# The triangular inversion inside a gated DeltaNet: 32-row substitution on VectorE, or 16-row substitution joined by small matmuls

## Chip, cores and metric

One of the eight cores of a Trainium2 chip runs the whole program. The metric is the device time of one execution in microseconds (us). Engines are named as the profile names them: PE is TensorE's matmul side and PEld its weight loads, DVE is VectorE, ACT ScalarE, POOL GpSimd, SP SyncE. PE, DVE, ACT and POOL each work through their own queue strictly in the order of the program; semaphores tie the queues together.

## The reference, cut to what matters

Two layers of a diffusion transformer over 512 latent and 256 context tokens. In each layer one half of the mixer is a gated DeltaNet with 8 heads, run forwards and backwards over chunks of 64 tokens. Each chunk, head and direction needs the solution of a unit lower triangular system of 64 rows:

```python
a_mat = jnp.where(strict, jnp.einsum('bhnid,bhnjd->bhnij', kb, k) * decay, 0.0)
eye = jnp.eye(CHUNK, dtype=jnp.float32)
rhs = jnp.concatenate([v * beta[..., None], kb * jnp.exp(gc)[..., None]], axis=-1)
sol = lax.linalg.triangular_solve(a_mat + eye, rhs, left_side=True, lower=True)
```

The kernel forms the inverse of `a_mat + eye` and multiplies with it. The other half of the mixer is latent attention; projections and a SwiGLU FFN surround both, for the context and the latent tokens.

## The kernel before

Each layer is written as several Python generators: input projection, the DeltaNet chain, the preparation and the body of attention, output projection with FFN, modulation. `weave` is a planner that picks which generator goes on next: every `yield` gives a span, a PE cost and a DVE cost, `TUNE` gives each stream a rank and a factor on those costs, and from them the order of all engines' instructions is fixed when the program is built. Nothing is reordered at run time.

`gdn_pre` prepares the DeltaNet for 16 units (head pair by chunk) in both directions. It runs six times: once over the context in each layer, and twice over the latent tokens in each layer (heads 0 to 3, then 4 to 7). Call these inversions 1 to 6; in order of time they are context layer 0, latent layer 0 twice, context layer 1, latent layer 1 twice. A tile holds on its 128 partitions four quarters of 32 rows (two heads, two 32-row diagonal blocks of the 64-row matrix) and along the free axis 32 units (16 units, two directions). The inversion goes so:

- The diagonal 32-blocks are gathered in `bd`, transposed to `L` (line 568), and `M` starts as the identity.
- The loop of lines 571 to 576 substitutes row by row: for `r` from 0 to 30, one multiply makes an outer product of `n` = 31 - r by `m` = r + 1 elements in `tmp` (shown as `st<-g,g`), one subtract takes it from `M` (shown as `g<-g,st`). That is 62 DVE instructions, all through the helper `tt` of line 139, each of which needs the one before it.
- Two transposes (lines 578, 579) turn `M` into `x1` and `x2`.
- Small matmuls of 32 x 32 (lines 587, 588, then 597, 598) join the two 32-blocks to a 64-block: 64 matmuls into one PSUM bank, a copy on ACT, 64 matmuls into another bank. Then come the products with values and keys (line 622) and the scan over chunks.

PSUM banks with the tag `B` hold these products; there are two, and attention's scores (line 961) use the same two. On PE the streams interleave: lines 221 and 226 are the projections and the FFN, 232 modulation and attention's output, 933, 938 and 946 the preparation of attention, whose maxima DVE reduces in lines 934 and 939. DVE also splits each weight tile in two (`wl<-wr,wh`, `fl<-fr,fh`). ACT runs every `cpy` and `act` through line 151.

Of the kernel before, what the change touches and what calls it, by code (L numbers as in the profile page):

```python
# [14 lines left out]
AF = mybir.ActivationFunctionType  # L15
# [5 lines left out]
P = 128  # L21
# [10 lines left out]
GROUPS = ((0, 4), (4, 4), (8, 4), (12, 4), (16, 3), (19, 3))  # L32
SLOT = 776

C_ID, C_BLK1, C_TRIF, C_TRIB, C_SEL, C_MSK, C_ONE, C_BLKM, C_QB = 0, 128, 256, 384, 512, 520, 524, 525, 527
NCONST = 529
B_MOD, N1, N2, CW, AL, DT, GN, QN, KN, FN = 0, 48, 56, 64, 124, 132, 140, 141, 143, 144
NSMALL = 152

# [66 lines left out]
def trunk_kernel(ctx, tc, xin, cc, wmod, small, win, wuq, wuk, wuv, wout, wgu, wdn, cst, rope, out):  # L106
    nc = tc.nc
    V, A, G, PE = nc.vector, nc.scalar, nc.gpsimd, nc.tensor
# [14 lines left out]
    def nm(s):  # L123
        uid[0] += 1
        return f"{s}_{uid[0]}"

    def slot(tag, dt=F32, w=None):
        width = WIDTH[tag]
        t = sp.tile([P, width], dt, name=nm(tag), tag=tag, bufs=BUFS[tag])
        return t[:, 0:w or width]  # L130

    def ps(tag):
        return pp.tile([P, 512], F32, name=nm("ps" + tag), tag=tag, bufs=PSB[tag])
# [4 lines left out]
    def tt(out, a, b, op=ALU.mult, e=None):  # L138
        (e or V).tensor_tensor(out=out, in0=a, in1=b, op=op)  # L139
# [7 lines left out]
    def stt(out, a, s, b, op0, op1):  # L147
        V.scalar_tensor_tensor(out=out, in0=a, scalar=s, in1=b, op0=op0, op1=op1)  # L148

    def act(out, a, f, **kw):  # L150
        A.activation(out, a, f, **kw)  # L151
# [4 lines left out]
    MUL, ADD, SUB = ALU.mult, ALU.add, ALU.subtract  # L156

    cct = cp.tile([P, KD, 2], F32, name="cct")
    nc.sync.dma_start(out=cct, in_=cc)
    cst_t = cp.tile([P, NCONST], F32, name="cst")  # L160
    nc.sync.dma_start(out=cst_t, in_=cst)
# [7 lines left out]
    sel = cst_t[:, C_SEL:C_SEL + 8]  # L169
    m0 = cst_t[:, C_MSK:C_MSK + 1]  # L170
    m1 = cst_t[:, C_MSK + 1:C_MSK + 2]
    nm0 = cst_t[:, C_MSK + 2:C_MSK + 3]
    nm1 = cst_t[:, C_MSK + 3:C_MSK + 4]
    ident_r = cp.tile([P, P], F32R, name="ident_r")
# [2 lines left out]
    for l in range(DEPTH):  # L177
        t = cp.tile([P, NSMALL], F32, name=f"small{l}")
# [266 lines left out]
    def st_tile():  # L445
        return slot("st")

    def u3(t):
        return t.rearrange("p (c i) -> p c i", i=64)
# [3 lines left out]
    def gdn_pre(l, st, hjs, kf, qf, vf, gt, res):  # L453
# [16 lines left out]
        for d in range(2):  # L470
            t = gb[d]
# [6 lines left out]
        def turned(f, a):  # L478
            pt = ps("B")
            for c in range(8):  # L480
                for hp in range(2):
                    s = slice(64 * hp, 64 * hp + 64)
                    PE.matmul(pt[s, 64 * c:64 * c + 64], u3(f)[s, a + c, :], ident[s, s], start=True, stop=True)
            return pt

        for a in (0, 8):
            pt = turned(kf, a)
# [20 lines left out]
        for a in (0, 8):  # L508
            pt = turned(vf, a)
# [20 lines left out]
        if full:  # L530
# [3 lines left out]
            pt = ps("B")  # L534
# [5 lines left out]
        for b in range(0, U, nb):  # L540
            pt = ps("B")
            pv = pt.rearrange("p (c z i) -> p c z i", z=nz, i=64)
# [14 lines left out]
        bd, L, M = (slot("g4") for _ in range(3))  # L557
# [4 lines left out]
        b3 = bd.rearrange("p (u i) -> p u i", i=32)  # L562
# [3 lines left out]
        V.transpose(out=bd[:, 512:1024], in_=bt)  # L566
        L3 = L.rearrange("p (i j) -> p i j", j=32)
        V.transpose(out=L3, in_=bd.rearrange("p (u i) -> p i u", i=32))
        M3 = M.rearrange("p (i j) -> p i j", j=32)
        tmp = slot("st", w=256)  # L570
        for r in range(31):
            n, m = 31 - r, r + 1
            t3 = tmp[:, 0:n * m].rearrange("p (a b) -> p a b", b=m)
            tt(t3, L3[:, r + 1:32, r:r + 1].to_broadcast([P, n, m]), M3[:, r:r + 1, 0:m].to_broadcast([P, n, m]))
            tt(M3[:, r + 1:32, 0:m], M3[:, r + 1:32, 0:m], t3, SUB)
            yield 1, 0, 0.5
        x1, x2 = bd, L
        V.transpose(out=x1.rearrange("p (u r) -> p r u", r=32), in_=M3)
        V.transpose(out=x2.rearrange("p (u s) -> p s u", s=32), in_=M.rearrange("p (r s) -> p s r", s=32))
        X1 = x1.rearrange("p (u r) -> p u r", r=32)  # L580
        X2 = x2.rearrange("p (u r) -> p u r", r=32)
        zp = ps("B")
        zv = zp.rearrange("p (c i) -> p c i", i=32)
        for c in range(U):
            for hp in range(2):
                r0, r1 = 64 * hp, 64 * hp + 32
                PE.matmul(zv[r1:r1 + 32, c, :], u3(bm[0])[r0:r0 + 32, c, 32:64], X2[r0:r0 + 32, c, :], start=True, stop=True, tile_position=(r0, r1))
                PE.matmul(zv[r0:r0 + 32, c, :], u3(bm[1])[r1:r1 + 32, c, 0:32], X1[r1:r1 + 32, U + c, :], start=True, stop=True, tile_position=(r1, r0))
        z = st_tile()
# [4 lines left out]
        for c in range(U):  # L594
            for hp in range(2):
                r0, r1 = 64 * hp, 64 * hp + 32
                PE.matmul(zv[r0:r0 + 32, c, :], z3[r1:r1 + 32, c, :], X1[r1:r1 + 32, c, :], start=True, stop=True, tile_position=(r1, r0))
                PE.matmul(zv[r1:r1 + 32, c, :], z3[r0:r0 + 32, c, :], X2[r0:r0 + 32, U + c, :], start=True, stop=True, tile_position=(r0, r1))
        vv = gb
        act(u3(vv[0])[:, :, 0:32], X1[:, 0:U, :], AF.Identity, scale=m0)  # L600
        act(u3(vv[0])[:, :, 32:64], X1[:, 0:U, :], AF.Identity, scale=m1)
        stt(u3(vv[0])[:, :, 32:64], zv, nm0, u3(vv[0])[:, :, 32:64], MUL, ADD)
        act(u3(vv[1])[:, :, 0:32], X2[:, U:2 * U, :], AF.Identity, scale=m0)
        act(u3(vv[1])[:, :, 32:64], X2[:, U:2 * U, :], AF.Identity, scale=m1)
        stt(u3(vv[1])[:, :, 0:32], zv, nm1, u3(vv[1])[:, :, 0:32], MUL, ADD)
# [6 lines left out]
        for dst, lh, rh in ((us, vv, (vs, vs)), (W, ke, vv)):  # L612
            for a in range(0, U, 4):
                pt = ps("B")
                pv = pt.rearrange("p (n d i) -> p n d i", d=2, i=64)
                for q in range(4):
                    n, hi = divmod(a + q, nh)
                    for d in range(2):
                        c = hi * nch + (nch - 1 - n if d else n)
# [189 lines left out]
    scale = 96.0 ** -0.5  # L809
# [249 lines left out]
    class Mix:  # L1059
# [55 lines left out]
        def stage(self, g):  # L1115
            f = self.f[g]
            if g in self.spilled:
                for kind in "kqv":
                    t = slot("g4")
                    nc.sync.dma_start(out=t.rearrange("p (j t) -> p j t", j=len(g)), in_=f[kind].rearrange("j p t -> p j t"))  # L1120
                    f[kind] = t
            return gdn_pre(self.l, self.st, g, f["k"], f.get("q"), f["v"], self.gates, self.pre[g])
# [202 lines left out]
    for k in range(KD):  # L1325
        t = slot("t", w=NL)
# [33 lines left out]
def _constants():  # L1360
    f = np.float32
    c = np.zeros((P, NCONST), f)
    p = np.arange(P)
    c[:, C_ID:C_ID + P] = np.eye(P, dtype=f)
    c[:, C_ONE] = 1.0 / D
    same = (p[:, None] // 64) == (p[None, :] // 64)
    c[:, C_BLKM] = (p < 64) / 64.0
    c[:, C_BLKM + 1] = (p >= 64) / 64.0
    c[:, C_BLK1:C_BLK1 + P] = same
    c[:, C_QB] = 64 * EPS * (p < 64)  # L1370
    c[:, C_QB + 1] = 64 * EPS * (p >= 64)
    c[:, C_TRIF:C_TRIF + P] = same & (p[:, None] <= p[None, :])
    c[:, C_TRIB:C_TRIB + P] = same & (p[:, None] >= p[None, :])
    for j in range(4):
        for r in range(2):
            c[32 * j + r, C_SEL + 2 * j + r] = 1.0
    first = (p // 32) % 2 == 0
    c[:, C_MSK] = first
    c[:, C_MSK + 1] = ~first
    c[:, C_MSK + 2] = -1.0 * first  # L1380
    c[:, C_MSK + 3] = -1.0 * ~first
    t = np.arange(NL)
    inv = f(10000.0) ** (-np.arange(0, 16, 2, dtype=f) / f(16))
    ang = []
    for pos in ((t // GRID_W).astype(f), (t % GRID_W).astype(f)):
        a = pos[:, None] * inv[None, :].astype(f)
        ang += [a, a]
    ang = np.concatenate(ang, axis=1).astype(f)
    sign = np.where((np.arange(32) % 16) < 8, -1.0, 1.0).astype(f)
    rope = np.concatenate([np.tile(np.cos(ang).T.astype(f), (4, 1)), np.tile(np.sin(ang).T * sign[:, None], (4, 1))], axis=1)  # L1390
    return c, rope
# [8 lines left out]
def _layout(i):  # L1400
# [19 lines left out]
    def heads(a):  # L1420
# [7 lines left out]
        [col(i["b_mod"], 48), col(i["norm1_g"], KD), col(i["norm2_g"], KD), cw, heads(i["a_log"]), heads(i["dt_bias"]),  # L1428
         gn, col(i["q_norm_g"], 2), col(i["kv_norm_g"], 1), fn], axis=2)
    o["cst"], o["rope"] = _constants()  # L1430
    return {k: np.ascontiguousarray(v) for k, v in o.items()}

# [16 lines left out]
```

## Time and profile before

| | |
|---|---|
| median of 3 runs | 2238.65 us (2234.93 to 2241.45) |
| profiled execution | 2228.82 us, of which span on the core 2227.0 us |
| PE busy, share of the span | 91% |
| DVE busy | 67% |
| ACT busy | 39% |
| mean granted clock of TensorE | 0.946 of 2.4 GHz |

Busy times say how long an engine had something in work. They are means over stages, so a stage is judged by its own window: how busy the engines were in it and what ended the waits of the engine that mattered.

### The profile page before, as it was taken

How to read it: one execution, taken by the hardware profiler on the slowest of the kernel's cores; microseconds unless marked ns; L12 is line 12 of the kernel's file. 1: busy time of each engine (PE TensorE's matmuls, PEld its weight loads, DVE VectorE, ACT ScalarE, POOL GpSimd, SP SyncE). 2: the span in 40 equal slices, each digit the busy share in tenths (PEclk: the TensorE clock that was granted, in tenths of full speed). 3: DMA queues.
4: the chain of work that ended last, by engine and by line, in shares of the span. 5: the costliest groups of instructions: out<-in, count | busy, mean ns of one | idle time of the engine just before them, and what ended most of it. 6: DMA issues, size and time to landing. Idle time of an engine off the chain costs nothing. (4 is left out here: it accounts for less than half of the span.)

```text
span 2227.0 us, 40577 instructions
## 1 busy us (share of the span) xinstructions
PE 2034.1 (91%) x16048; PEld 1592.5 (72%) x16048; DVE 1497.3 (67%) x2926; ACT 871.5 (39%) x1541; POOL 127.1 (6%) x283
## 2 busy tenths in 40 slices
PE   5999988889898999899999998987876988999996
PEld 3776677889895567788888876765544667888885
DVE  4779678986678787778454458887787555444445
ACT  3335375543443434553323244444322234223233
POOL 0200013000201000100000000200200000000000
PEclk8999998899999999999999999997986999999998
DMA  8345613343445402343223245521110022233332
GB/s 319 135 147 180 194 43 119 124 158 120 119 130 161 142 11 92 98 141 97 81 78 98 95 141 199 163 73 34 38 34 11 30 76 75 95 97 97 95 99 76
DMA packets 130638, 240.42 MB, mean 108 GB/s; under 512 B 15184, under 2 KB 30064, under 8 KB 130448
## 3 DMA queue, kind: packets, MB, share of 16 engines
q1 hardware_dynamic: 124592, 224.10, 30.9%
q0 software_dynamic: 5856, 13.74, 2.2%
q8 instruction: 126, 2.06, 0.4%
q14 instruction: 64, 0.52, 0.1%
HBM read 228.24 MB, written 6.91 MB: 106 GB/s over the span
## 5 line engine op out<-in xcount | busy, mean ns | idle before, releaser
L221 PE MATMUL psA<-hx,wh 128*128 128x512 f32 x1680 | 535.0, 398 | 20.2 <-ACT hx L151 8.5
L151 ACT ACTIVATE wh<-wr 128x512 fp32r<-128x512 f32 (+2 forms) x410 | 249.2, 608 | 650.6 <-PE psA L221 480.3
L139 DVE TENSOR_TENSOR wl<-wr,wh 128x512 fp32r<-128x512 f32 (+2 forms) x410 | 270.6, 661 | 231.7 <-ACT wh L151 231.3
L221 PEld LDWEIGHTS psA<-hx,wh 128*128 128x128 f32 x1680 | 314.5, 190 | 107.6 <-issue 12.4
L221 PE MATMUL psA<-hx,wl 128*128 128x512 f32 x840 | 330.7, 394 | 5.3 <-DVE wl L139 5.3
L221 PE MATMUL psM<-hx,wh 128*128 128x512 f32 x704 | 217.6, 390 | 0.0
L221 PEld LDWEIGHTS psA<-hx,wl 128*128 128x128 f32 x840 | 159.0, 189 | 42.2 <-DVE wl L139 8.3
L151 ACT ACTIVATE fh<-fr 128x512 fp32r<-128x512 f32 (+3 forms) x186 | 110.9, 600 | 156.6 <-PE psM L221 44.1
L148 DVE SCALAR_TENSOR_TENSOR g<-psA,mod,g 128x512 f32<-128x512 f32 x112 | 83.9, 749 | 105.8 <-PE psA L221 105.6
L221 PEld LDWEIGHTS psM<-hx,wh 128*128 128x128 f32 x704 | 132.3, 188 | 27.2
L139 DVE TENSOR_TENSOR fl<-fr,fh 128x512 fp32r<-128x512 f32 (+3 forms) x186 | 120.5, 653 | 39.2 <-ACT fh L151 37.7
L221 PE MATMUL psM<-hx,wl 128*128 128x512 f32 x352 | 137.0, 389 | 0.0
L221 PE MATMUL psF<-m,fh 128*128 128x256 f32 x600 | 117.3, 294 | 6.5 <-ACT tc L151 5.0
L221 PE MATMUL psA<-hd,wh 128*128 128x512 f32 x384 | 120.4, 392 | 0.0
L221 PEld LDWEIGHTS psF<-m,fh 128*128 128x128 f32 x600 | 96.2, 195 | 13.0 <-ACT tc L151 6.6
L221 PE MATMUL psA<-ox,wh 128*128 128x512 f32 x320 | 100.7, 393 | 0.0
L221 PE MATMUL psF<-m,fl 128*128 128x256 f32 x300 | 86.8, 289 | 4.4 <-DVE fl L139 4.2
L226 PE MATMUL psA<-m,g 128*128 128x256 f32 x320 | 75.8, 398 | 8.6 <-DMA g<-win 3.9
L221 PEld LDWEIGHTS psA<-hd,wh 128*128 128x128 f32 x384 | 71.7, 188 | 16.4 <-DVE hd L139 1.1
L221 PE MATMUL psM<-m,fh 128*128 128x256 f32 x416 | 81.3, 293 | 1.6 <-ACT m L151 0.9
L226 PEld LDWEIGHTS psA<-m,g 128*128 128x128 f32 x320 | 63.0, 199 | 19.6 <-ACT m L151 7.6
L221 PEld LDWEIGHTS psM<-hx,wl 128*128 128x128 f32 x352 | 66.1, 188 | 13.6
(382 smaller groups left out, 3704.0 us busy)
## 6 DMA issues: line engine op xcount, KB each, us to landing
wr<-wgu SPq DMA_DIRECT2D x176, 256.0 KB, 2.6
m<-wmod SPq DMA_DIRECT2D x160, 256.0 KB, 4.3
fr<-wgu SPq DMA_DIRECT2D x88, 256.0 KB, 2.8
wr<-win SPq DMA_DIRECT2D x80, 256.0 KB, 3.3
wr<-wdn SPq DMA_DIRECT2D x64, 256.0 KB, 2.6
g<-win SPq DMA_DIRECT2D x20, 512.0 KB, 7.2
g<-wmod SPq DMA_DIRECT2D x16, 512.0 KB, 10.2
fr<-wdn SPq DMA_DIRECT2D x32, 256.0 KB, 2.7
```

The lines of the kernel that those rows point to most:

```text
L139: (e or V).tensor_tensor(out=out, in0=a, in1=b, op=op)
L148: V.scalar_tensor_tensor(out=out, in0=a, scalar=s, in1=b, op0=op0, op1=op1)
L151: A.activation(out, a, f, **kw)
L221: PE.matmul(o, ww[:, wk], xx if n is None else xx[:, a:a + n], start=cnt == 0, stop=cnt == 3 * nk - 1)
L226: PE.matmul(o, w[:, k * P:k * P + P], x_, start=k == 0, stop=k == len(xs) - 1)
```

## The change

The substitution stops at blocks of 16 rows. Both 16-blocks of each 32-block are substituted by the same instructions (`corners` is a view of the two diagonal 16 x 16 corners), so 15 rows remain, 30 instructions. Then PE joins the two 16-blocks: `blocks` multiplies 64 tiles of 32 x 32 into one bank, four at a time on the four diagonal positions of the array. It is called six times per inversion. Two calls form the product of the block below the diagonal (kept in `b3`, the rest of which a memset and a multiplication by the mask `m16` clear) with `x2`; ACT copies both into `M`. Four calls multiply from the other side, once for `x2` and once for `x1`, and DVE subtracts each result from its half of `x2` or `x1`. `x1` and `x2` now lie in `L` and `kf`, so that `bd` can keep the block below the diagonal.

```diff
         L3 = L.rearrange("p (i j) -> p i j", j=32)
         V.transpose(out=L3, in_=bd.rearrange("p (u i) -> p i u", i=32))
+        G.memset(b3[:, :, 0:16], 0.0)
+        act(b3[:, :, 16:32], b3[:, :, 16:32], AF.Identity, scale=m16)
         M3 = M.rearrange("p (i j) -> p i j", j=32)
-        tmp = slot("st", w=256)
-        for r in range(31):
-            n, m = 31 - r, r + 1
-            t3 = tmp[:, 0:n * m].rearrange("p (a b) -> p a b", b=m)
-            tt(t3, L3[:, r + 1:32, r:r + 1].to_broadcast([P, n, m]), M3[:, r:r + 1, 0:m].to_broadcast([P, n, m]))
-            tt(M3[:, r + 1:32, 0:m], M3[:, r + 1:32, 0:m], t3, SUB)
-            yield 1, 0, 0.5
-        x1, x2 = bd, L
+
+        def corners(t):
+            return bass.AP(t.tensor, t.offset, [t.ap[0], [16 * 33, 2], [32, 16], [1, 16]])
+
+        L4, M4 = corners(L), corners(M)
+        tmp = slot("st", w=128)
+        for r in range(15):
+            n, m = 15 - r, r + 1
+            t4 = tmp[:, 0:2 * n * m].rearrange("p (z a b) -> p z a b", z=2, b=m)
+            tt(t4, L4[:, :, r + 1:16, r:r + 1].to_broadcast([P, 2, n, m]), M4[:, :, r:r + 1, 0:m].to_broadcast([P, 2, n, m]))
+            tt(M4[:, :, r + 1:16, 0:m], M4[:, :, r + 1:16, 0:m], t4, SUB)
+            yield 1, 0, 0.4
+        x1, x2 = L, kf
...
+        quads = [slice(32 * g, 32 * g + 32) for g in range(4)]
+
+        def blocks(u, lh, rh):
+            pt = ps("B")
+            pv = pt.rearrange("p (u i) -> p u i", i=32)
+            for c in range(16):
+                for g, q in enumerate(quads):
+                    PE.matmul(pv[q, c, :], lh[q, u + c, :], rh[q, u + c, :], start=True, stop=True, tile_position=(32 * g, 32 * g))
+            return pt
+
+        for u in (0, 16):
+            cpy(M[:, 32 * u:32 * u + 512], blocks(u, b3, X2))
+            yield 2, 1.2, 0
+        for u in (0, 16):
+            c = slice(32 * u, 32 * u + 512)
+            pn, pt = blocks(u, X1, M3), blocks(u, M3, X1)
+            tt(x2[:, c], x2[:, c], pn, SUB)
+            tt(x1[:, c], x1[:, c], pt, SUB)
+            yield 3, 2, 1.4
```

The costs in the `yield` lines differ, so the planner's order differs from inversion 1 on. PE's queue in inversion 4 (context, layer 1) had this before; `hd` and `ox` are inputs of other streams' matmuls (line 221, psA) and the small matmuls stand in pairs:

```order
L221 MATMUL psA_11678<-hd_11568,wh_11650 128x512
L221 MATMUL psA_11678<-hd_11569,wh_11650 128x512
L221 MATMUL psA_11678<-hd_11568,wl_11651 128x512
L587 MATMUL psB_11696<-g_2027_11072,g_1926_10534 32x32
L588 MATMUL psB_11696<-g_2026_11071,g_1927_10535 32x32
...
L221 MATMUL psA_11840<-ox_11414,wl_11675 128x512
L597 MATMUL psB_11763<-g_2026_11071,st_11761 32x32
L598 MATMUL psB_11763<-g_2027_11072,st_11761 32x32
```

Now the same place reads so (line 597 is the matmul in `blocks`, 614 and 615 are the old 587 and 588, 222 is the old 221; 48 of its matmuls stand between each two groups of blocks):

```order
L597 MATMUL psB_12436<-g_1874_11226,g_2044_12169 32x32 x64
L222 MATMUL psA_12526<-hx_10948,wh_12352 128x512
...
L222 MATMUL psM_12527<-hx_10990,wl_12371 128x512
L597 MATMUL psB_12584<-g_1874_11226,g_2044_12169 32x32 x64
L597 MATMUL psB_12650<-g_2046_12171,g_2045_12170 32x32 x64
L597 MATMUL psB_12715<-g_2045_12170,g_2046_12171 32x32 x64
L222 MATMUL psA_12806<-hx_10948,wh_12504 128x512
...
L222 MATMUL psM_12807<-hx_10990,wl_12523 128x512
L597 MATMUL psB_12864<-g_2046_12171,g_2045_12170 32x32 x64
L597 MATMUL psB_12929<-g_2045_12170,g_2046_12171 32x32 x64
L614 MATMUL psB_12996<-g_1874_11226,g_1944_11632 32x32
```

Six groups of 64 small matmuls have come in, and the first old one (614), which reads the results of DVE's last subtractions, stands right behind the last of them.

On DVE the second place is the end of inversion 6 (last of layer 1). Before, the substitution's rows stood between the maxima (934) of attention's preparation up to the transposes:

```order
L934 TENSOR_REDUCE mx_17213<-psA_17217 128x1
L139 TENSOR_TENSOR g_3096_16949<-g_3096_16949,st_16959 128x7x25
L139 TENSOR_TENSOR st_16959<-g_3095_16948,g_3096_16949 128x156
L934 TENSOR_REDUCE mx_17213<-psA_17220 128x1
L139 TENSOR_TENSOR g_3096_16949<-g_3096_16949,st_16959 128x6x26
...
L578 STREAM_TRANSPOSE g_3094_16947<-g_3096_16949 128x32x32
L579 STREAM_TRANSPOSE g_3095_16948<-g_3096_16949 128x32x32
```

Now the next four maxima (961) and two more (966) stand between the subtractions of the joins:

```order
L587 STREAM_TRANSPOSE g_2723_16032<-g_3109_18712 128x32x32
...
L961 TENSOR_REDUCE mx_19025<-psA_19026 128x1
L961 TENSOR_REDUCE mx_19025<-psA_19029 128x1
L139 TENSOR_TENSOR g_2723_16032<-g_2723_16032,psB_19056 128x512
L961 TENSOR_REDUCE mx_19025<-psA_19032 128x1
L961 TENSOR_REDUCE mx_19025<-psA_19035 128x1
L139 TENSOR_TENSOR g_3108_18711<-g_3108_18711,psB_19121 128x512
L966 TENSOR_REDUCE mx_19025<-psA_19038 128x2
...
L139 TENSOR_TENSOR g_3108_18711<-g_3108_18711,psB_19257 128x512
```

A set of maxima that used to follow the substitution now shares the queue with the joins.

## Rows read from the trace of the kernel before

**Rows 1.** The page's busy times with shares, and the granted clock in 40 slices.

```profile
PE 2034.1 (91%) x16048; PEld 1592.5 (72%) x16048; DVE 1497.3 (67%) x2926; ACT 871.5 (39%) x1541; POOL 127.1 (6%) x283
...
PEclk8999998899999999999999999997986999999998
```

**Rows 2.** Windows, one per inversion: length, busy PE, PEld, DVE, ACT, POOL, PEclk, DMA, GB/s.

```profile
168.90:282.40 113.50, 107.50 (x739) 76.69 (x738) 88.47 (x185) 49.37 (x89) 6.96 (x22) 0.95 0.57 186
398.80:501.60 102.80, 90.55 (x896) 84.38 (x895) 88.80 (x199) 50.44 (x91) 0.00 (x0) 0.93 0.43 138
653.30:734.40 81.10, 70.43 (x630) 47.64 (x629) 67.80 (x151) 30.55 (x59) 5.94 (x11) 0.89 0.52 165
1000.30:1076.20 75.90, 75.90 (x579) 62.47 (x578) 57.54 (x117) 24.48 (x40) 0.00 (x0) 1.00 0.31 98
1461.80:1505.00 43.20, 35.14 (x394) 23.82 (x392) 36.25 (x86) 19.82 (x32) 0.00 (x0) 0.88 0.14 46
1645.20:1718.00 72.80, 47.67 (x376) 26.53 (x375) 60.47 (x127) 19.04 (x33) 1.94 (x4) 0.67 0.05 15
```

**Rows 3.** Groups by line on DVE: busy us, mean ns, idle before.

```profile
L139 DVE TENSOR_TENSOR g<-g,st 128x31 f32<-128x31 f32 (+15 forms) x186 | 63.2, 340 | 3.4
L139 DVE TENSOR_TENSOR st<-g,g 128x31 f32<-128x31 f32 (+15 forms) x186 | 63.0, 339 | 3.2
...
L139 DVE TENSOR_TENSOR g<-psB,sv 128x512 f32<-128x512 f32 x12 | 8.1, 685 | 0.1
```

**Rows 4.** Timeline of DVE in inversion 5: start us, us, instruction.

```profile
1464.32 0.20 DVE L139 TENSOR_TENSOR st<-g,g 128x31 f32<-128x31 f32 x1
...
1478.57 0.42 DVE L139 TENSOR_TENSOR st<-g,g 128x256 f32<-128x256 f32 x1
1479.03 0.42 DVE L139 TENSOR_TENSOR g<-g,st 128x256 f32<-128x256 f32 x1
...
1492.07 0.19 DVE L139 TENSOR_TENSOR g<-g,st 128x31 f32<-128x31 f32 x1
1492.29 1.91 DVE L578 STREAM_TRANSPOSE g<-g 128x1024 f32<-128x1024 f32 x1
```

**Rows 5.** Groups by line on PE, 1071.8 to 1076.3 us (two records a matmul).

```profile
L588 PE MATMUL psB<-g,g 32*32 32x32 f32 x64 | 1.3, 193 | 0.0
...
L587 PE MATMUL psB<-g,g 32*32 32x32 f32 x64 | 1.3, 193 | 0.0
```

**Rows 6.** Groups by line on PE, 1496 to 1498.2 us, inversion 5.

```profile
L587 PE MATMUL psB<-g,g 32*32 32x32 f32 x64 | 1.9, 236 | 5.5 <-issue 5.5
```

**Rows 7.** Groups by line on ACT and POOL: busy us, mean ns, idle before.

```profile
L151 ACT ACTIVATE g<-psB 128x512 f32<-128x512 f32 x60 | 35.5, 592 | 32.5 <-PE psB L622 18.7 <-PE psB L483 13.5
...
L151 ACT ACTIVATE g<-g,cst 128x512 f32<-128x512 f32 x24 | 17.2, 718 | 23.2 <-DVE g L578 8.1 <-PE psB L588 5.3 <-DVE g L579 5.1
...
L560 POOL MEMSET g<- 128x1024 f32 x6 | 5.8, 975 | 0.0
```

**Rows 8.** Waits of PE in the windows of inversions 1, 2, 3: us, times, longest.

```profile
PE psA L221 <- DVE wl L139: 3.5, 1, 3.5
...
PE psF L221 <- DVE tc L148: 2.2, 2, 1.2
PE psF L221 <- DVE fl L139: 2.0, 2, 1.0
...
PE psF L221 <- DVE fl L139: 1.8, 1, 1.8
PE psA L933 <- DVE mx L934: 1.2, 1, 1.2
```

**Rows 9.** Waits of PE in the window of inversion 6.

```profile
PE psA L933 <- DVE mx L934: 5.0, 6, 1.5
PE psA L221 <- DVE hd L139: 3.8, 1, 3.8
PE psA L938 <- DVE mx L939: 2.4, 3, 0.8
```

More of the change, by code (lines that the diff above doesn't have):

```diff
@@ L33 @@
 SLOT = 776
-C_ID, C_BLK1, C_TRIF, C_TRIB, C_SEL, C_MSK, C_ONE, C_BLKM, C_QB = 0, 128, 256, 384, 512, 520, 524, 525, 527
-NCONST = 529
+C_ID, C_BLK1, C_TRIF, C_TRIB, C_SEL, C_MSK, C_ONE, C_BLKM, C_QB, C_M16 = 0, 128, 256, 384, 512, 520, 524, 525, 527, 529
+NCONST = 530
 B_MOD, N1, N2, CW, AL, DT, GN, QN, KN, FN = 0, 48, 56, 64, 124, 132, 140, 141, 143, 144
@@ L171, in trunk_kernel @@
     m1 = cst_t[:, C_MSK + 1:C_MSK + 2]
+    m16 = cst_t[:, C_M16:C_M16 + 1]
     nm0 = cst_t[:, C_MSK + 2:C_MSK + 3]
@@ L1381, in _constants @@
     c[:, C_MSK + 3] = -1.0 * ~first
+    c[:, C_M16] = (p % 32) < 16
     t = np.arange(NL)
```

## The prediction

> **What bounds the kernel now.** I read the page first. PE is busy for 91% of the span, DVE for 67% [rows 1], so PE is the first suspect, and a change that gives PE work to spare DVE starts with a debt. A mean says nothing about the stages, so I cut one window for each of the six inversions, from the transpose ahead of the substitution to the last old join matmul [rows 2]. The reader is to look at length minus PE busy, and at DVE beside it. Inversions 1 to 3: PE idle 6.0, 12.3 and 10.7 us, DVE busy 78%, 86% and 84%. Inversion 4: PE idle 0.0, so here PE alone sets the time. Inversion 5: idle 8.1 of 43.2, DVE 84%. Inversion 6: idle 25.1 of 72.8, DVE 83%, granted clock 0.67. The first four are (almost) full on PE, the last two are paced by DVE and by trips between engines.
>
> Third, the waits of PE in these windows. In inversions 1 to 3 the longest that DVE ended are 3.5, 2.2, 2.0, 1.8 and 1.2 us, together 10.7 [rows 8]: DVE delivers split weights (`wl`, `fl`) or FFN rows late. In inversion 6 they are 5.0, 3.8 and 2.4, together 11.2 [rows 9]. In inversion 5 PE stands 5.5 us ahead of the first join matmul [rows 6]; the releaser is not given, but the two transposes stand on DVE just then [rows 4].
>
> **What is removed from DVE.** The two groups of the substitution take 63.2 + 63.0 us over six inversions [rows 3], 21.0 each. Sizes: 31 elements take 0.19 us, 256 take 0.42 [rows 4], so 1.02 ns per element and 0.16 us fixed; and two neighbours start 0.46 apart, 0.04 more than one lasts. Old: 62 instructions, 2 x 5456 elements = 62 x 0.16 + 11.1 = 21.0, which agrees. New: 30 instructions over 2 x 1360 elements (both corners; the sum over m of 2m(16 - m), twice) = 30 x 0.16 + 2.8 = 7.6. That saves 13.4 busy and, with 32 gaps of 0.04, 14.7. Four subtractions of 128x512 from PSUM come in, priced by the like product from PSUM at 0.685 [rows 3]: 2.7. Net relief of DVE: 10.7 us busy, 11.8 with gaps (14.7 - 2.7 - 4 x 0.04), per inversion. The four-dimensional views have no row here; if each instruction paid another 0.1 us, 3 us of it would be gone.
>
> **What is added to PE.** Six groups of 64 matmuls per inversion. The old joins are the same work: 64 matmuls of 32x32 on four positions of the array, whose two lines alternate in the program; both take the same 1.3 us at full clock [rows 5], 1.9 us where inversion 5 runs below it [rows 6]. So 7.8 us in inversion 4. For 1 to 3, with clocks of 0.95, 0.93 and 0.89 [rows 2], I put 1.4 a group, 8.4 each. Inversions 1 to 4: 3 x 8.4 + 7.8 = **+33.0**. Inversions 5 and 6: 6 x 1.9 = 11.4 each, counted below.
>
> Here a rule is weighed. The Trainium skill (TensorEngine Tiling (Array Packing), Restrictions and Gotchas) says that different row tiles cannot access the same PSUM bank at the same time; `blocks` writes four row tiles into one bank. By that, its matmuls would go one by one. The trace disagrees: lines 587 and 588 also fill one bank from four row tiles, and 64 matmuls (128 records of 193 ns each) are through in 1.3 us [rows 5]. The sum goes by the row; the rule's result is the last rival.
>
> **What DVE's relief gives back in 1 to 3.** At least nothing; at most all PE idle of the three windows, 6.0 + 12.3 + 10.7 = 29.0. I take the waits that DVE visibly ended, **-10.7**: with 11.8 us less in each queue these have reason to go, while the rest is ended by ACT, DMA or in bits below 1.2 us. In 4 there is nothing to give back.
>
> **The new waits on PE.** PE stands in order, so each group of blocks that waits holds up every stream's matmuls behind it. In the order shown for inversion 4, 48 matmuls of another stream stand between the first, second and third batch, so ACT's copies (0.59 each [rows 7]) and the first subtractions have cover, unless DVE runs late by more than those matmuls take. No cover stands between the last two groups and line 614, which needs the last two subtractions: 2 x 0.685 = 1.4 us, four times, **+5.6**. Below that it can be 0, if DVE catches up; above, the longest such wait in the trace is 5.5 [rows 6], 22 for four. The mask on ACT (0.72) and the memset on POOL (1.0 for a tile twice as large [rows 7]) lie beside the substitution; if POOL or ACT were late, the first group of blocks would wait about 1 us more.
>
> **Inversion 5.** Substitution and what DVE does between its rows run from 1464.32 to 1492.29 [rows 4]. This gets 14.7 shorter. The joins follow in series, with hardly anything of other streams between: two groups 3.8, one copy 0.6, two groups 3.8, two subtractions 1.4 (both banks are taken till then), two groups 3.8, two subtractions 1.4, together 14.8 at the low clock and 11.2 at full clock. Net between -3.5 and +0.1; I put **0** and bounds of -6 and +6, because the planner moves other work too.
>
> **Inversion 6.** PE idles 25.1 us [rows 2], so 11.4 of joins fit in if they come at the right moment. The new order puts them among the maxima of attention's preparation, the place where PE waits for DVE [rows 9]. The relief is at most 11.8, at least 0, since the subtractions now queue with the maxima. Two thirds, **-8**: the waits that DVE ends amount to 11.2, nearly the whole relief, but the joins add trips between PE and DVE.
>
> **Sum.** 33.0 - 10.7 + 5.6 + 0 - 8 = +19.9 us. On the profiled execution that is 2228.8 + 19.9 = 2248.7; this execution lies 9.8 us below the median of the three runs, 2238.65, and the same difference on the median gives 2258.6, so **2258 us**. The ends: 33 - 29 + 0 - 6 - 11.8 = -14 (2225) and 33 - 0 + 22 + 6 - 0 = +61 (2300).
>
> **The rivals.**
>
> *DVE sets the pace of the four inversions with idle, and the change is faster.* For it: DVE is at 78% to 86% wherever PE has idle, and PE's share overstates its load, since weight loads are busy for only 72% [rows 1]. Against: inversion 4 has no gap on PE, and only 10.7 of 29.0 idle in 1 to 3 is visibly DVE's. If all that idle returns and 5 and 6 gain DVE's full relief: 33 - 29 - 2 x 11.8 = -20, 2219 us. It decides once more than some 33 us come back. The Trainium skill (Perfetto Trace Analysis, Identifying the Most-Contended Engine) leans this way: matmul busy share is a bad measure of distance to the limit, weight-load share a better one. By it inversion 4 would have 13.4 us of PE to spare (62.5 of 75.9) and its joins would cost nothing, 7.8 less in the sum; the rows show no gap there into which they could fall.
>
> *The joins make PE wait.* Three dependencies per inversion run through the queues of DVE and ACT, with two `psB` banks that attention shares. If two of them cost the 5.5 us of [rows 6] in each of 1 to 4, that is 44 instead of 5.6: +58, 2297. For it: DVE's queue is full in these windows. Against: the cover of 48 matmuls.
>
> *It comes out even.* Cost and relief differ by less than 6.7 us, 0.3% of the median and about what a measurement of this kernel can tell from nothing. This needs about 13 us more returned than I put; 2240.
>
> *Small tiles go one at a time.* Then a group costs four times 1.3: 36 x 3.9 = 140 more, 2399. Rows 5 speak plainly against it.
>
> **How the numbers follow.** PE pays (my forecast): 0.50, its own range 2246 to 2275. Faster: 0.21. Joins wait: 0.12. Even: 0.15. One at a time: 0.02. The time is that of the likeliest. The range leaves out about half of the faster case below and the upper ends above: 2227 to 2288. Slower by over 0.3%: 0.50 + 0.12 + 0.02 = 0.64; within: 0.15; faster: 0.21.
>
> **What would show it.** The new L597 on PE with 4608 records and groups of 64 matmuls near 1.3 us in inversion 4; the substitution at some 45 us in all instead of 126; PE's busy time up by 45 to 60 us and its idle in the windows of 1 to 3 down by some 10; a wait of about 1.4 us ahead of 614. Wrong would be: subtractions or products far above 0.25 us on average, PE's waits ahead of 597 or 614 in tens of us, or a PE that gets its 33 us into idle that I took for bound. Most likely to mislead me is the planner: with other costs in the `yield` lines it weaves the whole program differently, and a stretch far from any inversion may open or close gaps that no row here prices.

## The result: 5.6% slower, and the profile after

The changed kernel takes 2363.82 us in the median of 4 runs (2361.62 to 2369.56), the kernel before 2239.14 beside it; the ratio is 1.0563, its interval 1.0538 to 1.0588. That is +125 us, where +20 was forecast, and outside the range. The profiled execution has a span of 2363.3 us. The first lines of its page, which answer to [rows 1], read:

```profile
PE 2126.4 (90%) x20656; PEld 1669.7 (71%) x20656; DVE 1449.2 (61%) x2758; ACT 885.2 (37%) x1559; POOL 129.0 (5%) x289
...
q8 instruction: 162, 2.65, 0.5%
```

PE is busy 92.3 us longer and DVE 48.1 us less, but PE's share has gone down: the span of the profiled execution grew by 136.3, so PE has also 44 us more idle. (That the span grew by more than the 125 us of the medians is because the profiled execution before was a short one.) The last line counts the packets that brought instructions. Its line before, important further down, is:

```profile
q8 instruction: 126, 2.06, 0.4%
```

The terms that the prediction priced locally are nearly all as priced. The groups of DVE and PE by line:

```profile
L139 DVE TENSOR_TENSOR g<-g,st 128x30 f32<-128x30 f32 (+7 forms) x90 | 22.6, 251 | 1.6
L139 DVE TENSOR_TENSOR st<-g,g 128x30 f32<-128x30 f32 (+7 forms) x90 | 22.6, 251 | 1.8
L139 DVE TENSOR_TENSOR g<-g,psB 128x512 f32<-128x512 f32 x24 | 16.3, 684 | 27.7 <-PE psB L597 24.8 <-PE psB L614 2.9
...
L597 PE MATMUL psB<-g,g 32*32 32x32 f32 x4608 | 59.0, 209 | 39.2 <-issue 29.6
```

The substitution takes 45.2 us in all (126.2 in [rows 3]), 7.5 per inversion. A subtraction takes 0.684. The 4608 records of the joins (two a matmul) keep PE busy for 59.0 us, 1.6 per group. The new thing stands at the end of the last row: PE idled 39.2 us just ahead of these matmuls, and 29.6 of that is put down to "issue", time in which it waited for nothing that the profile shows.

The windows of the inversions, first transpose to last old join, columns as in [rows 2]; the last row is a stretch that follows inversion 3:

```profile
172.30:290.00 117.70, 101.26 (x1410) 74.11 (x1409) 72.92 (x139) 44.42 (x76) 4.81 (x18) 0.91 0.47 158
422.20:514.00 91.80, 82.35 (x1472) 74.69 (x1471) 64.92 (x141) 45.22 (x88) 0.53 (x1) 0.83 0.33 106
654.50:725.00 70.50, 57.18 (x1346) 54.35 (x1345) 43.18 (x91) 25.76 (x46) 1.05 (x2) 0.88 0.34 108
1112.40:1184.20 71.80, 65.04 (x1241) 52.73 (x1240) 37.32 (x71) 19.85 (x32) 0.53 (x1) 0.90 0.22 72
1595.90:1657.30 61.40, 49.90 (x1176) 36.22 (x1174) 37.93 (x77) 27.20 (x43) 1.04 (x2) 0.86 0.16 49
1779.90:1835.00 55.10, 37.00 (x1084) 25.23 (x1083) 32.90 (x71) 13.10 (x23) 1.57 (x4) 0.66 0.07 22
727.00:957.00 230.00, 202.36 (x1608) 131.36 (x1607) 147.86 (x273) 88.19 (x164) 10.18 (x19) 0.90 0.31 100
```

Two things are to be seen. PE's idle inside the windows of 1 to 3 did not fall: 16.4, 9.5 and 13.3 us, against 6.0, 12.3 and 10.7 in [rows 2]; and inversion 4, which had none, has 6.8. Yet inversion 3 ends at 725 us, 9 us earlier than before (734.4). The loss shows behind it: the last row is the stretch in which attention of layer 0 runs, 230 us to its end at 957. Before, that attention ended at 850, after a stretch of 115 us:

```profile
735.00:850.00 115.00, 108.35 (x1104) 67.10 (x1103) 89.08 (x168) 51.77 (x95) 3.89 (x8) 1.00 0.21 64
```

So the end of layer 0's attention has already moved by 107 of the 136 us, and the prediction had not priced that stretch. Two theories came from this. JOINS: the joins cost it, by their work on PE and by waits. ORDER: the new costs in the `yield` lines cost it, because the planner lays the streams out differently.

### The profile page after: what moved, and what is told of

The parts are those of the page before. It is cut to its first block, busy times and chain, and to the rows that moved or that the text cites. A ratio compares the mean times of both kernels' runs of the same rounds, so it can differ in the third digit from the quotient of the medians.

```text
span 2363.3 us, 49670 instructions
## 1 busy us (share of the span) xinstructions
PE 2126.4 (90%) x20656; PEld 1669.7 (71%) x20656; DVE 1449.2 (61%) x2758; ACT 885.2 (37%) x1559; POOL 129.0 (5%) x289
## 4 chain that ended last, share of the span: by engine, by line
PE 67%; DVE 9%; ACT 3%; issue 3%; DMA 2%; DVEq 0%; SPq 0%; POOL 0%; ACTq 0%; POOLq 0%
PE psA L222 28%; PE psM L222 14%; PE psF L222 5%; PE psB L988 3%; PE psA L233 2%; PE psB L597 2%; PE psB L649 2%; DVE g L148 1%; ACT t L151 1%; PE psA L960 1%; PE psC L696 1%; PE psM L233 1%; PE psC L708 1%; PE psC L719 1%; DVE fl L139 1%
## 5 line engine op out<-in xcount | busy, mean ns | idle before, releaser
L222 PE MATMUL psA<-hx,wh 128*128 128x512 f32 x1680 | 548.9, 406 | 19.6 <-ACT hx L151 8.7
L222 PEld LDWEIGHTS psA<-hx,wh 128*128 128x128 f32 x1680 | 322.2, 194 | 112.0 <-issue 12.3
L222 PE MATMUL psA<-hx,wl 128*128 128x512 f32 x840 | 336.7, 401 | 5.3 <-DVE wl L139 4.5
L597 PE MATMUL psB<-g,g 32*32 32x32 f32 x4608 | 59.0, 209 | 39.2 <-issue 29.6
L597 PEld LDWEIGHTS psB<-g,g 32*32 32x32 f32 x4608 | 52.7, 120 | 52.3 <-issue 48.3
L222 PEld LDWEIGHTS psA<-hd,wh 128*128 128x128 f32 x384 | 71.9, 188 | 16.2 <-DVE hd L139 0.7
```

The source lines that it names most:

```text
L222: PE.matmul(o, ww[:, wk], xx if n is None else xx[:, a:a + n], start=cnt == 0, stop=cnt == 3 * nk - 1)
L597: PE.matmul(pv[q, c, :], lh[q, u + c, :], rh[q, u + c, :], start=True, stop=True, tile_position=(32 * g, 32 * g))
```

## Experiments

"Old yields" or "new yields" below means what the planner is given. The same yields give nearly, not exactly, the same order of the other streams: leaving out the 32 x 32 matmuls, PE's records in e3 below stand in the order of the kernel before up to the 950th of 14512, and 2190 places differ in all.

### Work and yields apart: four kernels

**e1**: new work, old yields (15 for the rows, 4 behind each of the four steps of the joins). **e2**: old work, new yields.

```diff
--- the new kernel
+++ e1
-            yield 1, 0, 0.4
+            yield 1, 0, 0.5
...
-            yield 2, 1.2, 0
+            for _ in range(4):
+                yield 1, 0, 0.5
...
-            yield 3, 2, 1.4
+            for _ in range(4):
+                yield 1, 0, 0.5
--- the old kernel
+++ e2
-            yield 1, 0, 0.5
+            if r % 2 and r < 30:
+                yield 1, 0, 0.4
...
+        for _ in range(2):
+            yield 2, 1.2, 0
+        for _ in range(2):
+            yield 3, 2, 1.4
         zp = ps("B")
```

**e3** is e1 and **e4** the new kernel with the joins left out: their yields stay, the blocks, copies, subtractions, mask and memset go.

> The new work, but weave is given the 31 old yields of every inversion, with their old costs: 15 for the rows, 4 after each of the four steps of the joins. Theory ORDER (the other yields let the planner lay out all streams differently, and that costs most of the 125 us): near my local sum, 2258 us, at least below 2290. Theory JOINS (joins, their waits and the clock they lower cost it wherever they stand): 2330 to 2370, as the changed kernel.

> The old 31 rows and no joins, but weave is given the 19 new yields with the new costs (two rows to a yield). ORDER: 2310 to 2350. JOINS: 2235 to 2255, as before.

> As e1, with the joins left out altogether (no blocks, copies, subtractions, mask or memset; the inverse lacks the block below the diagonal of each 32-block), 31 old yields. It shows what DVE's relief is worth alone. ORDER and JOINS alike: 2215 to 2235; the difference to e1 is the whole price of the joins in the old plan, 33 to 45 us by ORDER, 100 or more by JOINS.

> As the changed kernel with the joins left out altogether (the inverse lacks the block below the diagonal of each 32-block), its 19 yields kept. ORDER: 2300 to 2325, since the plan stays bad. JOINS: 2215 to 2240.

Measured medians in us, with the kernel before at 2238.77:

| | old work | 16 rows, no joins | 16 rows and joins |
|---|---|---|---|
| old yields | 2238.8 | 2218.1 (e3) | 2303.3 (e1) |
| new yields | 2291.7 (e2) | 2270.9 (e4) | 2363.8 (the change) |

Ratios to the kernel before: e1 1.0279 (1.0258 to 1.0300), e2 1.0219 (1.0195 to 1.0243), e3 0.9892 (0.9865 to 0.9919), e4 1.0132 (1.0107 to 1.0158). The table is nearly additive, so each edit has a price of its own: the relief of DVE is worth 20.7 and 20.9 us (column one to two), the joins cost 85.2 and 92.9 (two to three), the new yields 52.9, 52.7 and 60.5 (row one to two). With the old yields the change is +64.5, and the yields bring the rest of the 125. Both theories are half right: e1, e2 and e4 fell between the two expectations, and e3, where both said the same, met it.

How PE spends these prices can be read from the pages of e3, e1 and e2 (spans 2215.4, 2301.3 and 2290.0 us):

```profile
PE 2038.3 (92%) x16048; PEld 1598.6 (72%) x16048; DVE 1429.6 (65%) x2734; ACT 872.2 (39%) x1541; POOL 125.6 (6%) x283
```

```profile
PE 2097.4 (91%) x20656; PEld 1650.2 (72%) x20656; DVE 1446.1 (63%) x2758; ACT 884.8 (38%) x1559; POOL 128.8 (6%) x289
```

```profile
PE 2064.6 (90%) x16048; PEld 1614.7 (71%) x16048; DVE 1494.9 (65%) x2926; ACT 873.0 (38%) x1541; POOL 125.6 (5%) x283
```

From e3 to e1 the joins add 59.1 us of busy PE and 26.8 of idle, so in sum none of their work on PE went into idle time that was there without them. From the kernel before to e2 PE has the same 16048 records, yet is busy 30.5 us longer and idle 32.5 longer, at a mean granted clock of 0.926 for 0.946. From e3 to e4 (PE busy 2057.2 us of 2267.3) it is 18.9 and 33.0. So a third to a half of what the new yields cost is the same work at a lower clock, and the rest is idle.

### What the joins cost: e7, e8, e6, e9

The idle named "issue" had a pattern. PE's timeline in the changed kernel, inversion 5:

```profile
1625.62 1.51 PE L597 MATMUL psB<-g,g 32*32 32x32 f32 x153
1629.02 1.35 PE L597 MATMUL psB<-g,g 32*32 32x32 f32 x128 [1.89 <-issue]
1632.49 1.93 PE L597 MATMUL psB<-g,g 32*32 32x32 f32 x128 [2.12 <-issue]
1636.51 0.75 PE L597 MATMUL psB<-g,g 32*32 32x32 f32 x37 [2.09 <-issue]
...
1640.66 2.03 PE L597 MATMUL psB<-g,g 32*32 32x32 f32 x215
1645.35 0.52 PE L597 MATMUL psB<-g,g 32*32 32x32 f32 x37 [2.66 <-issue]
```

It runs 128 records, stands about 2 us, and runs 128 again, and the stops are not where a group begins. The instruction queue's packets in the same stretch (start in us, ns, bytes) are:

```
1626.69   945  16384
1630.14   958  16384
1634.21   958  16384
1637.69  1329  16384
1642.88   876  16384
```

The stops at 1627.13, 1630.36 and 1634.42 end 1.9 to 2.1 us later, each 2.3 us after a packet of 16384 bytes has started. Of the idle named "issue" ahead of line 597, every stop of 1 us or more in the changed kernel, 14 of them, ends 2.2 to 2.9 us after the start of a packet. A group of `blocks` is 128 records and 128 weight loads; six groups in six inversions are 36 groups, and the packet count has risen by 162 - 126 = 36. One group, one packet. The Trainium skill (Runtime: NRT & Kernel Launch, Instruction fetch mechanics) says that instructions come in blocks of 16 KiB, 256 of them, which fits these numbers; it adds that the fetch is mostly hidden, and here it is not, with 29.6 us of PE idle. That made a theory FETCH, and as its rival DEPENDENCE, that the waits are for DVE and ACT.

**e7** puts six groups per inversion on a finished tile into e3; nobody reads the results. **e8** has 15 long matmuls instead.

```diff
+        k3 = kt.rearrange("p (u i) -> p u i", i=32)
+        for n, u in ((1, 0), (1, 16), (2, 0), (2, 16)):
+            for _ in range(n):
+                pv = ps("B").rearrange("p (u i) -> p u i", i=32)
+                for c in range(16):
+                    for g in range(4):
+                        q = slice(32 * g, 32 * g + 32)
+                        PE.matmul(pv[q, c, :], k3[q, u + c, :], k3[q, u + c, :], start=True, stop=True, tile_position=(32 * g, 32 * g))
...
+        for n, u in ((2, 0), (3, 512), (5, 0), (5, 512)):
+            for i in range(n):
+                PE.matmul(ps("B"), ident, kt[:, u:u + 512], start=True, stop=True)
```

**e6** is e1 with its 16 yields inside the groups, behind every fourth or eighth column. **e9** is e1 with `ps("C")` in `blocks`, the banks of the scan.

> As e3 (no joins, old yields; the inverse lacks the block below the diagonal of each 32-block), plus six groups of 64 small matmuls per inversion that read a finished tile and whose results nobody reads. FETCH: 2285 to 2305, nearly the whole price of the joins without a single dependence. DEPENDENCE: 2218 + 53 of PE work = 2265 to 2275.

> As e7, with 15 matmuls of 128x128 by 512 columns in place of the 384 small ones in each inversion, about the same 8.1 us of PE in 30 records instead of 768. FETCH: 2262 to 2272, 20 to 35 us below e7. DEPENDENCE: the same as e7.

> As e1, with the 16 yields of the joins between the columns of the groups (each quarter or half group), so that other streams' long matmuls can come between. FETCH: 2270 to 2290, as the packets land under the long matmuls. Theory DEPENDENCE (the waits ahead of the joins are for DVE's subtractions and ACT's copies): 2300 or more, since the chain has the same steps and ends later.

> The new work in the old plan, with the six groups written into the two banks of the scan (tag C) instead of the two that attention and the old joins use (tag B). If the 36 us that the joins cost above the dummies are waits for a free bank: 2275 to 2290 instead of 2303. If they are the steps of the chain and the instruction packets: 2295 to 2308.

Measured: e8 2252.2 (1.0060, 1.0041 to 1.0080), e7 2267.5 (1.0129, 1.0107 to 1.0151), e6 2294.2 (1.0239, 1.0213 to 1.0264), e9 2299.6. PE's matmuls in question by line, e8 first, then e7, e1 and e6:

```profile
L590 PE MATMUL psB<-g,cst 128*128 128x512 f32 x180 | 85.5, 600 | 0.1
```

```profile
L595 PE MATMUL psB<-g 32*32 32x32 f32 x4608 | 58.2, 201 | 16.2 <-issue 16.1
```

```profile
L597 PE MATMUL psB<-g,g 32*32 32x32 f32 x4608 | 54.9, 201 | 36.3 <-issue 27.8 <-DVE g L587 8.6
```

```profile
L597 PE MATMUL psB<-g,g 32*32 32x32 f32 x4608 | 58.3, 198 | 20.4 <-issue 12.2 <-DVE g L587 7.9 <-DVE g L139 0.3
```

PE's totals in e8 and e7 (spans 2250.4 and 2266.1):

```profile
PE 2090.0 (93%) x16228; PEld 1613.5 (72%) x16228; DVE 1430.3 (64%) x2734; ACT 871.2 (39%) x1539; POOL 125.8 (6%) x283
```

```profile
PE 2092.0 (92%) x20656; PEld 1643.4 (73%) x20656; DVE 1430.5 (63%) x2734; ACT 871.4 (38%) x1539; POOL 126.2 (6%) x283
```

The 85 us of the joins come apart in two steps. The small matmuls alone, e3 to e7: +49. PE is busy 53.7 us longer and idle 3.0 less, so the stops took the place of other idle. The dependences, e7 to e1: +36, of which 29.8 are idle and 5.4 busy. In e1 the idle named "issue" is 27.8 against 16.1 in e7, so some 12 of these 36 are packets too: the real joins stand closer together than the dummies.

e8 was meant as the work of e7 in few instructions, and is not an equal control. Its matmuls keep PE busy for 85.5 us, those of e7 for 58.2, and its mean granted clock is higher (0.961 against 0.949). The two come out even in PE's total, 2090.0 and 2092.0, and the 15 us between the two runs are nearly all idle, 160.4 against 174.1. That is near the 16.2 us ahead of e7's small matmuls, all but 0.1 of it "issue", with nothing to depend on. So FETCH is shown as a cause of the stops; about 15 us for what they cost e7 is an estimate from an uneven pair.

Spread over the other streams (e6) the issue idle falls by 15.6 to 12.2, the time only by 9, and the intervals of e6 and e1 just overlap. The expectations: e7 met that of DEPENDENCE and lay below that of FETCH; e8 and e6 met neither, e8 below both and e6 between them. The shared banks are not the cause: e9's ratio is 1.0268 (1.0251 to 1.0285) and e1's 1.0279 (1.0258 to 1.0300). What the other 24 or so of the 36 are, waits of PE for the transposes (8.6 in e1) or a chain that ends later, stays open.

### Which inversions pay: e5, g2, g1

Old yields throughout. **e5** has the new work in inversions 5 and 6 alone, **g2** in 6 alone (`if l == 1 and st is LAT and hjs[0] == 2`). **g1** is e5 with four groups, `x2` by a transpose, and the yields inside the groups as in e6:

```diff
+                    if c % 4 == 3:
+                        yield 1, 0, 0.5
...
-                pn, pt = blocks(u, X1, M3), blocks(u, M3, X1)
-                tt(x2[:, c], x2[:, c], pn, SUB)
+                pt = yield from blocks(u, M3, X1)
                 tt(x1[:, c], x1[:, c], pt, SUB)
+            V.transpose(out=x2, in_=x1)
```

> The new work in inversions 5 and 6 alone (latent tokens, layer 1), the old work in 1 to 4, the old yields everywhere. My prediction gave these two 0 and -8 us: 2231. Theory FETCH (each run of small matmuls stands 2.0 to 2.7 us whenever it has used up a 16 KB packet of instructions, beside its work on PE): 2245 to 2262, a third of the 65 us that all six cost in the old plan.

> The new work in inversion 6 alone, old yields. My prediction gave -8: 2231. If inversion 6 is where PE's idle takes in the joins, at most 2240; if both share the 7 us of inversions 5 and 6: 2241 to 2244.

> As the run with the new work in inversions 5 and 6 alone, but only x1 is joined on PE (four groups per inversion instead of six, spread by quarter groups) and x2 is made from it by one more transpose on DVE of 2.0 us. FETCH: two packets fewer per inversion and half of the rest covered, 5 to 8 us below 2246, so 2236 to 2242, even with the kernel before. If the chain of steps sets the price: 2244 to 2250.

e5 takes 2245.6 (ratio 1.0027, 1.0013 to 1.0041), g2 2239.9 (0.9998, 0.9983 to 1.0014), g1 2237.8 (0.9998, 0.9984 to 1.0012). So inversion 6, where PE idles, loses nothing and gains nothing: its joins take what the relief of DVE gives there. Inversion 5 loses some 6 us (the intervals of e5 and g2 just touch), and inversions 1 to 4 cost 2303.3 - 2245.6 = 58. g1 brings 5 and 6 back to even; whether the fewer groups do it or the spread yields was not tried apart.

### Where the yields cost: f1, f2, h1, h2

Old work; the new yields in one part of the six inversions, by a flag ahead of the loop, as `new = l == 1`. **f1**: inversion 1. **f2**: 2 to 6. **h1**: layer 1. **h2**: layer 0.

> Old work everywhere; the new yields in inversion 1 alone (context, layer 0). Theory FIRST (the context's attention behind inversion 1 falls back in the order, its FFN with it, and latent attention then runs with nothing beside it): most of the 53 us that the new plan costs, 2275 to 2295. Rival SUM (each inversion's yields cost a little): 2243 to 2253.

> Old work everywhere; the new yields in inversions 2 to 6. FIRST: 2235 to 2255. SUM: 2275 to 2290.

> Old work; the new yields in the three inversions of layer 1 alone. Theory LAYER0 (the new order costs only by pushing layer 0's latent attention behind the DeltaNet work it used to run beside): 2232 to 2245, as before. Rival EVERYWHERE (each stretch with another order loses some): 2250 to 2265.

> Old work; the new yields in the three inversions of layer 0 alone. LAYER0: 2282 to 2297, all of the 53 us. EVERYWHERE: 2265 to 2278.

f1 2277.5 (1.0187, 1.0155 to 1.0218), f2 2264.1 (1.0122, 1.0099 to 1.0145), h1 2234.5 (0.9978, 0.9963 to 0.9993), h2 2291.8 (1.0233, 1.0216 to 1.0250). f1 and f2 do not add up: 39 + 26 us, where both together (e2) cost 53. f1 met FIRST, and f2 lies between FIRST and SUM, so neither theory holds as it stood. h1 and h2 settle the place: all 53 us lie in layer 0; in layer 1 the new yields are worth 0.2%. Where in layer 0 shows first in attention's reciprocal, which ends one head pair: eight times, four per layer; the row gives the first and last start. Kernel before, then h1, h2 and the changed kernel:

```profile
L978 DVE RECIPROCAL t<-psA x8: 3350/3357/3358, 730.8 to 1781.8; 128x512 f32<-128x512 f32 x8
```

```profile
L987 DVE RECIPROCAL t<-psA x8: 3347/3356/3358, 738.4 to 1787.5; 128x512 f32<-128x512 f32 x8
```

```profile
L987 DVE RECIPROCAL t<-psA x8: 3357/3357/3359, 786.6 to 1836.2; 128x512 f32<-128x512 f32 x8
```

```profile
L1005 DVE RECIPROCAL t<-psA x8: 3344/3357/3358, 843.7 to 1919.5; 128x512 f32<-128x512 f32 x8
```

With the new yields in layer 0 the first head pair is done 55.8 us later, and the last of layer 1 54.4 later: nothing more is lost in layer 1. But a late head pair is not all loss, since other work now stands ahead of it. The loss is placed by stretches in which PE does about the same work (busy time times granted clock). First the kernel before, then h2:

```profile
262.00:450.00 188.00, 165.96 (x1997) 142.18 (x1994) 146.74 (x324) 103.41 (x204) 26.77 (x44) 0.89 0.32 100
450.00:781.00 331.00, 308.57 (x3627) 259.09 (x3627) 253.09 (x526) 142.20 (x259) 24.25 (x39) 0.96 0.44 138
781.00:861.00 80.00, 74.52 (x640) 48.36 (x640) 66.65 (x132) 35.92 (x65) 0.14 (x3) 1.00 0.10 34
```

```profile
266.00:477.00 211.00, 174.96 (x2006) 149.75 (x2004) 157.67 (x355) 105.92 (x208) 26.21 (x44) 0.83 0.30 89
477.00:805.00 328.00, 308.88 (x3719) 265.51 (x3721) 233.09 (x504) 131.86 (x238) 22.05 (x35) 0.96 0.44 133
805.00:916.00 111.00, 89.85 (x306) 49.49 (x301) 76.01 (x123) 45.87 (x85) 2.37 (x11) 0.80 0.15 46
```

There are two losses, 23 us from the end of inversion 1 on and 31 at the end of attention, and none between. Both show more idle of PE (36.0 for 22.0, 21.2 for 5.5) and a lower granted clock. Cut likewise, f1 loses 21 us in the first stretch and 18 in the last, f2 none and 34; so the first loss is inversion 1's, the last comes from either, which is why they do not add up. In the first stretch one wait can be named. Ahead of a matmul of the context's attention (psF, line 855 in h2) PE waits for DVE to write the keys `kc`: 9.9 us in h2 and 11.7 in f1, and below 1 us in the kernel before, f2 and h1. That is the attention that FIRST spoke of; the rest of the 23 us stays open.

What the last loss stands beside shows in one window of e2, 700 to 909 us, in which latent attention runs:

```profile
700.00:909.00 209.00, 182.89 (x1238) 112.01 (x1238) 132.09 (x248) 76.22 (x141) 10.17 (x19) 0.86 0.33 101
```

and in a window of equal length of the kernel before, 640 to 851:

```profile
640.00:851.00 211.00, 193.56 (x1886) 127.93 (x1885) 170.49 (x349) 86.79 (x161) 9.99 (x19) 0.96 0.33 104
```

In about 210 us the old order got 1886 PE records (256 of them small join matmuls) and 170 us of DVE work done, the new one 1238 and 132, at a granted clock of 0.86 for 0.96. In the old order attention ran beside the third inversion and the scan, which ends at 829, 21 us ahead of attention's end. In the new one the inversion is over (the old kernel's last join matmuls of inversion 3 end at 734, e2's at 684) before the first scores at 702, and the scan ends at 757. From there to its end at 914 attention has no DeltaNet matmuls beside it, with trips to ACT and DVE between. That this is the cause of the last loss is argued from these rows; no run put the work back beside it. Which of the yields' numbers moves it, the shorter total or the PE costs, was not tried.

### Together: h3 and h4

**h3** is h1 with g1's work (four groups, x2 by a transpose) in inversions 5 and 6, under the new yields. **h4** repeats h1 beside it.

> Layer 0 with old work and old yields; layer 1 with the new yields, and in inversions 5 and 6 the 16-row substitution with four groups of joins and one more transpose. If the new yields of layer 1 (2234.5 alone) and the cheaper joins (even with before) add up: 2230 to 2236, faster than before. If the joins take back what the order gives: 2237 to 2245.

> The old work with the new yields in layer 1 alone, a second time: 2230 to 2237 if its 0.2% is real, 2237 to 2241 if not.

h3: 2237.6 (0.9980, 0.9964 to 0.9995); h4: 2235.5 (0.9978, 0.9965 to 0.9991); the kernel before beside them 2240.5. The gain of 0.2% came twice (h1, h4), with intervals that end below 1, and comes from the order of layer 1. It is there without the joins, and the joins add nothing to it that can be told from noise.

## Why the prediction was wrong

- **The sum** is the step that failed first: it had no term for the order. New yields alone cost 53 us (e2), all in layer 0 (h1, h2), a third to a half of it as the same work at a lower clock, the rest as idle of PE. The text had named the planner as most likely to mislead, and gave it no price and no place in the range.
- **The new waits on PE** were mis-sized and misplaced. Forecast were 5.6 us ahead of line 614; there 1.7 are lost. Measured were 36 to 39 us ahead of the small matmuls themselves, 28 to 30 of them "issue", and 26.8 us of idle in all (e3 to e1). The price of 1.3 us a group came from single old groups [rows 5]; six close together use up their instructions faster than packets arrive. No row ahead of the prediction showed it: before the 5.5 us of issue in [rows 6] the last packet had started 18.1 us earlier, so they were no such stop; the second transpose ends at 1496.0, just ahead of the first join at 1496.1, and the reading as a wait for the transposes stands.
- **What is added to PE** was right: 33.0 + 22.8 = 55.8 us forecast, 59.0 measured (54.9 in e1). In inversion 6 it was to fit into idle time; over all six it did not (e3 to e1).
- **What is removed from DVE** was right: 7.6 us a substitution forecast, 7.5 measured; 0.685 a subtraction, 0.684 measured.
- **The relief given back** was of the right kind: 20.7 us over all six (e3). I put 10.7 on 1 to 3, and there the profile of e3 shows no gain: at the same point of PE's work it is at 1604 us, the kernel before at 1590. It gains 27 us around inversion 6, where the granted clock rises too. The kernel before, then e3:

```profile
1590.00:1728.00 138.00, 98.97 (x875) 60.25 (x875) 105.99 (x210) 42.29 (x71) 14.13 (x15) 0.74 0.08 25
```

```profile
1604.00:1715.00 111.00, 87.58 (x906) 55.45 (x900) 87.71 (x165) 40.30 (x70) 13.38 (x18) 0.83 0.09 27
```

- **Inversions 5 and 6** were mis-sized: 0 and -8 forecast, about +6 and 0 measured. Inversions 1 to 4 cost 58 in the old order, where 33.0 - 10.7 + 5.6 = 27.9 was forecast.
- **The rivals.** The one with waiting joins (2297) has the right kind of loss and comes near the old-order run (2303), though with another cause than DVE's queue for part of it; the 2363.8 it does not reach, as it has no order either. By its number alone small tiles one at a time (2399) is nearer, and that would be luck, for it stays refuted: 128 records of line 597 are through in 1.3 us in the changed kernel too, in this row of 1137 to 1139 us:

```profile
L597 PE MATMUL psB<-g,g 32*32 32x32 f32 x128 | 1.3, 193 | 0.0
```

## What to carry to other kernels

Where a planner sets the order, a changed cost in its input is an edit of its own: split it from the work by giving the old work the new costs and the new work the old ones, and the table says which of the two one is looking at. Work in very many tiny instructions has a price beside its busy time; multiply its instructions by their size and ask how fast they can be brought. Spreading them over other work took away more than half of that idle here (27.8 to 12.2 us), but only 9 of the joins' 85 us.

## What was not expected of the hardware

PE used up a 16384-byte packet of instructions (128 matmul records with their weight loads) in 1.3 us, and then stood 1.9 to 2.7 us until the next had come (inversion 5 of the changed kernel); packets started 3.5 to 4.1 us apart in such a run. Long matmuls in the same places had 0.1 us of idle ahead of them (e8), small ones 16.2 (e7).
